# A gate joined behind its projection, memory tiles split in pairs, high and low parts by pairs of weight pieces

## The chip, the cores and the metric

The kernel runs on one core of a Trainium2 chip (trn2). The metric is the device time of one execution in microseconds; the median of several runs is given. TensorE (PE) does the matmuls and transposes, ScalarE (ACT) activations and copies, VectorE (DVE) elementwise work and reductions, SyncE (SP) issues the DMAs. Matmuls accumulate in PSUM, which is divided into banks.

## The reference

A decoder layer on 256 tokens of width 4096, in fp32. One input projection feeds three groups of heads, whose outputs are gated by SiLU, joined, projected, normalised and added to the residual.

```python
h = rms_norm(x, g_pre)
p = h @ w_in
p_shift = token_shift(p[..., :RWKV_SHIFT_WIDTH], mu_rwkv)
r, k, v, wl, al = jnp.split(p_shift, _offsets(RWKV_SHIFT_SPLITS), axis=-1)
g_rwkv, fq, fk, fv, f_logit, g_fox, mq, g_mq = jnp.split(p[..., RWKV_SHIFT_WIDTH:], _offsets(REST_SPLITS), axis=-1)
y_rwkv = rwkv7_branch(r, k, v, wl, al, w0, w_decay_up, a0, w_iclr_up, k_k, k_a, r_k, ln_x_w, ln_x_b)
log_f = jax.nn.log_sigmoid((f_logit + b_f).astype(jnp.float32)).transpose(0, 2, 1)
y_fox = fox_attention(to_heads(fq), to_heads(fk), to_heads(fv), log_f)
y_mem = memory_cross_attention(mq, mem, g_mem, w_mem_kv)
y = jnp.concatenate([y_rwkv * jax.nn.silu(g_rwkv), y_fox * jax.nn.silu(g_fox),
                     y_mem * jax.nn.silu(g_mq)], axis=-1)
y = y @ w_out
return x + rms_norm(y, g_post)
```

`rwkv7_branch` is a recurrence over the tokens for 24 heads of 64, with a norm for each head. `fox_attention` is causal softmax attention of 24 heads of 64 with a forget gate, and the memory attention has 4 heads of 256 over 256 memory tokens.

## The kernel before

**High and low parts.** Every operand of a big product is split into a high part (fp32r, a rounded copy) and a low part (what is left), so that a product is three matmul terms: high x high, high x low, low x high. `wsplit` (L211) loads a weight piece of 128 x 1024 by a DMA on SP's queue into one of four raw buffers, writes the high part `wh` on ACT (L217) and the low part `wl` on DVE (L218); each has three buffers.

**Projections.** `proj_t` makes 128 outputs of a projection for all 256 tokens, in 110 places of the program. Its 4096 inputs are 32 tiles of 128, its weights four pieces of eight tiles. The activations `xs` (`ms` for the memory) hold a tile's high and low part beside each other, so one matmul of 512 columns with `wh` (L248) gives two terms, and one of 256 columns with `wl` (L251) the third. For each piece come eight high matmuls and then eight low ones; in the last piece one high matmul stands at the very end, as it closes the sum. The sum stands in a PSUM tile of the pool `pj`, which has two banks. `join` adds its two halves: a copy on ACT (L262) and an addition on DVE (L264, or L266 where there is a scale); after that the bank is free.

**Names.** `pjq6400f` and `pjq7936f` are the banks of the query and key projections of a pair of fox heads, `pjgf` that of its gate, `pjgr` that of an RWKV gate; numbers behind the names are the pair (`f2`) or group and pair (`r02`). `pn` are the sums of `proj_n`, where the weights move and the activations stand (the memory values `pnmv`, the fox values, the output `pno`). `sf` are a pair's scores, `Lf` its logits and probabilities, `tf` and `of` the transposes and outputs; `mpr` and `vvr` are sums over a head for the RWKV norm; `yp` are the split tiles of the output projection's input, made from `y` (L896, L897).

**Order of the work.** After the memory phase (memory values, eight memory key projections `mk`, then queries and gates) come three groups of four pairs. A group runs four RWKV pairs, the recurrence, the fox values, and then fox pairs 0 to 3 with the norms between them: norms 0 and 1 are written behind fox pair 0, norm 2 behind fox pair 1, norm 3 behind fox pair 2. `rwkv_norm` (L732) sums the heads, projects the gate `gtr` and joins it into a tile with two buffers (tag `gt`); `put_y` (L339) reads the gate. The code is recorded in this order and a scheduler, which goes by its own estimate of each instruction's time, chooses the order on each engine when the program is built; weight loads and splits go ahead by a priority. On the chip each engine then works through its fixed order and waits by semaphores.

Of the kernel before, what the change touches and what calls it, by code (L numbers as in the profile page):

```python
# [8 lines left out]
F32 = mybir.dt.float32  # L9
F32R = mybir.dt.float32r  # L10
AF = mybir.ActivationFunctionType
ALU = mybir.AluOpType
# [3 lines left out]
P = 128  # L16
T = 256
D = 4096
KT = D // P
# [13 lines left out]
O_GR, O_FQ, O_FK, O_FV, O_FL, O_GF, O_MQ, O_GM = (  # L33
    4864, 6400, 7936, 9472, 11008, 11032, 12568, 13592)
# [110 lines left out]
def f32(ap):  # L145
    return ap.bitcast(F32)


class Layer:
# [86 lines left out]
    def proj_t(self, key, xs, name):  # L236

        nc = self.nc
        i = W_INDEX[key]
        ps = self.pj.tile([P, 512], F32, tag="pj", name=f"pj{name}")  # L240
        for j in range(4):
            with self.tc.high_priority(offset=self.ahead):
                wh, wl = self.wsplit(self.a["wT"][i, :, 8 * j:8 * j + 8, :], [P, 8, P], f"{name}_{j}")
            def mul(u, k):

                x = xs[(8 * j + k) // 2][:, (8 * j + k) % 2]
                if u == 0:
                    self.late = nc.tensor.matmul(ps, wh[:, k, :], x.rearrange("p u t -> p (u t)"),  # L248
                                                 start=(j == k == 0), stop=(j == 3 and k == 7))
                else:  # L250
                    nc.tensor.matmul(ps[:, 0:T], wl[:, k, :], x[:, 0, :], start=False, stop=False)  # L251


            last = j == 3
            for u, k in [(0, k) for k in range(8 - last)] + [(1, k) for k in range(8)] + [(0, 7)] * last:
                mul(u, k)
        return ps

    def join(self, ps, out, scale=1.0):
# [84 lines left out]
    def mem_phase(self):  # L344
        nc, tc, a = self.nc, self.tc, self.a
        with tc.tile_pool(name="pm", bufs=2) as pm:
            ms = [self.slot(f"m{i}") if i < 8 else
                  pm.tile([P, 2, 2, T], F32R, tag="ml", name=f"m{i}", bufs=8) for i in range(16)]

            def split(i, src, g, ds, rb):  # L350

                raw = pm.tile([P, 4, T], F32, tag="xraw", name=f"{g}raw{i}", bufs=3)
                nc.sync.dma_start(raw, src[:, 4 * i:4 * i + 4, :])
                if rb is not None:
                    for k in range(4):
                        m = nc.vector.scalar_tensor_tensor(raw[:, k, :], raw[:, k, :], self.prm(g, 4 * i + k), rb,
                                                           ALU.mult, ALU.mult)
                        self.behind(m, self.joined)
                for k in range(4):
                    sc = self.prm(g, 4 * i + k)  # L360
                    h, l = (ds[2 * i + k // 2][:, k % 2, u, :] for u in range(2))
                    if rb is None:
                        nc.scalar.activation(h, raw[:, k, :], AF.Copy, scale=sc)
                        nc.vector.scalar_tensor_tensor(l, raw[:, k, :], sc, f32(h), ALU.mult, ALU.subtract)
                    else:
                        nc.scalar.activation(h, raw[:, k, :], AF.Copy)
                        nc.vector.tensor_tensor(l, raw[:, k, :], f32(h), ALU.subtract)

            raw0 = [pm.tile([P, 4, T], F32, tag="xraw", name=f"firstraw{i}", bufs=3) for i in range(2)]

            def split_one(k, w):
# [7 lines left out]
                nc.vector.scalar_tensor_tensor(l, raw, sc, f32(h), ALU.mult, ALU.subtract)  # L379
                return h, l  # L380

            nc.scalar.dma_start(self.par, a["par"])
            mk = [pm.tile([P, 4, T], F32, name=f"mk{i}", bufs=1) for i in range(2)]
            mv = [pm.tile([P, 4, T], F32, name=f"mv{i}", bufs=1) for i in range(2)]
            ahead, self.ahead = self.ahead, 0
            for i in range(2):
                pre = (lambda kt: kt % 4 == 0 and split(kt // 4, a["memT"], "g_mem", ms, None)
                       ) if i == 0 else None
                ps = self.proj_n(a["wN"][i], ms, f"mv{i}", pre, i == 0, first=split_one if i == 0 else None)
                self.ahead = ahead  # L390
                for t in range(2):

                    o = mv[t].rearrange("p a b -> p (a b)")[:, 512 * i:512 * i + 512]
                    nc.scalar.activation(o, ps[t], AF.Copy)
# [11 lines left out]
            def x_piece(i):  # L406
                self.xs += [self.slot(f"x{2 * i}"), self.slot(f"x{2 * i + 1}")]
                split(i, a["xT"], "g_pre", self.xs, rxb)

            for i in range(8):  # L410
                ps = self.proj_t(("mem", 128 * i), ms, f"mk{i}")
# [8 lines left out]
            for h in range(4):  # L420
                q = pm.tile([P, 2, T], F32, tag="q", name=f"mq{h}", bufs=2)
                g = pm.tile([P, 2, T], F32, tag="g", name=f"mg{h}", bufs=2)
                for j in range(2):
                    ps = self.proj_t(("in", O_MQ + 256 * h + 128 * j), self.xs, f"mq{h}{j}")
                    self.join(ps, q[:, j, :], 1.0 / 16.0)
                for j in range(2):
                    ps = self.proj_t(("in", O_GM + 256 * h + 128 * j), self.xs, f"gm{h}{j}")
# [4 lines left out]
                for t in range(2):  # L432
                    for j in range(2):
                        c = 2 * h + j
                        nc.tensor.matmul(sv[:, t, :], q[:, j, P * t:P * t + P], mk[c // 4][:, c % 4, :],
                                         start=(j == 0), stop=(j == 1))
# [295 lines left out]
    def rwkv_norm(self, g, p, G, pr):  # L732

        nc = self.nc
        kp = GP * g + p
        n = f"r{g}{p}"
        Y, bv = G["Y"], G["bv"]

        def f(name, shape=(P, T)):
            return pr.tile(list(shape), F32, tag="f", name=f"{name}{n}", bufs=3)  # L740

        mp = self.head_sums(Y[:, p, :], f"mp{n}", "ch", pr, "f")
        yc = Y[:, p, :]
        nc.vector.scalar_tensor_tensor(yc, mp, -1.0 / HD, Y[:, p, :], ALU.mult, ALU.add)
        sq = f("ysq")
        nc.scalar.activation(sq, yc, AF.Square)

        gt = pr.tile([P, T], F32, name=f"gt{n}", tag="gt", bufs=2)
        gp = self.proj_t(("in", O_GR + 128 * kp), self.xs, f"g{n}")
        vp = self.head_sums(sq, f"vv{n}", "ch", pr, "f", self.late)  # L750
        self.join(gp, gt)
        nc.scalar.activation(gt, gt, AF.Silu)
        sd = f("sd")
        nc.scalar.activation(sd, vp, AF.Sqrt, bias=self.eps[:, 1:2], scale=1.0 / HD)
        nc.vector.reciprocal(sd, sd)
        nc.vector.tensor_tensor(yc, yc, sd, ALU.mult)
        nc.vector.tensor_scalar(yc, yc, self.prm("ln_x_w", kp), self.prm("ln_x_b", kp), ALU.mult, ALU.add)
        nc.vector.tensor_tensor(yc, yc, bv[p], ALU.add)
        self.put_y(kp, yc, gt, pr)
# [203 lines left out]
```

## Time and profile before

| what | value |
|---|---|
| time, median of 3 runs | 1980.67 us (1980.45 to 1981.16) |
| time of the profiled execution | 1980.58 us |
| its span in the trace | 1978.8 us |
| mean granted clock of TensorE | 0.996 of full |
| TensorE busy | 1955.3 us, 99% |
| DVE, ACT busy | 1324.5 us (67%), 1043.0 us (53%) |
| DMA moved | 382.75 MB, 193 GB/s on the mean |

The span is the stretch that the trace covers; 1.8 us of the execution lie around it. A busy engine is one that has an instruction running. The granted clock is TensorE's, as a share of its full 2.4 GHz.

### The profile page before, as it was taken

What the parts mean: (1) busy time and instruction counts of PE and PEld (TensorE: products, weight loads), DVE (VectorE), ACT (ScalarE), POOL (GpSimd) and SP (SyncE); (2) the same over time, 40 slices, a digit from 0 to 9 for tenths busy, and PEclk for the clock granted to TensorE, in tenths of its full rate; (3) what the DMA queues carried; (4) which work ended last, traced back from release to release, by engine and by line L of the source; (5) the groups of instructions that cost most, each with busy time, mean ns of one, the idle gap of its engine ahead of it and who ended that gap; (6) DMA issues with size and microseconds to landing.
All of it is one profiled execution on the core that took longest, in us unless ns stands there. A gap on an engine that the chain in (4) does not pass through costs nothing.

```text
span 1978.8 us, 30221 instructions
## 1 busy us (share of the span) xinstructions
PE 1955.3 (99%) x11772; PEld 1669.0 (84%) x11772; DVE 1324.5 (67%) x1904; ACT 1043.0 (53%) x1460; POOL 36.0 (2%) x138
## 2 busy tenths in 40 slices
PE   9999999999999999999999999999999999999997
PEld 7888888888888888888888888888888888888886
DVE  6467444458889656678897576778975675444445
ACT  7745544445554456565545565655445664444443
POOL 0000000000000000000000000000000001000000
PEclk9999999999999999999999999999999999999999
DMA  9966555665556555655565556556555578666665
GB/s 367 332 206 212 167 177 180 181 197 179 178 165 186 171 155 176 189 182 172 171 190 165 162 177 187 180 179 176 179 165 154 161 242 301 198 201 200 198 196 181
DMA packets 113283, 382.75 MB, mean 193 GB/s; under 512 B 12764, under 2 KB 19316, under 8 KB 113140
## 3 DMA queue, kind: packets, MB, share of 16 engines
q1 hardware_dynamic: 111204, 374.44, 61.1%
q0 software_dynamic: 1792, 6.29, 0.9%
q8 instruction: 92, 1.51, 0.3%
q14 instruction: 51, 0.42, 0.1%
q10 hardware_dynamic: 144, 0.10, 0.0%
HBM read 372.89 MB, written 7.89 MB: 192 GB/s over the span
## 4 chain that ended last, share of the span: by engine, by line
PE 97%; DMA 1%; DVE 1%; ACT 0%; issue 0%; SPq 0%; DVEq 0%; ACTq 0%
PE pno L284 6%; PE pno L285 6%; PE pno L283 6%; PE pjq7936f L248 5%; PE pjq6400f L248 5%; PE pjgf L248 5%; PE pjgr L248 5%; PE pjvr L248 4%; PE pjrr L248 4%; PE pjkr L248 4%; PE pjmq L248 3%; PE pjgm L248 3%; PE pjmk L248 3%; PE pjgr L251 2%; PE pjq7936f L251 2%; PE pjgf L251 2%
## 5 line engine op out<-in xcount | busy, mean ns | idle before, releaser
L218 DVE TENSOR_TENSOR wlno<-rawno,whno 128x1024 fp32r<-128x1024 f32 x128 | 156.6, 1225 | 161.6 <-ACT whno L217 161.6
L217 ACT ACTIVATE whno<-rawno 128x1024 fp32r<-128x1024 f32 x128 | 135.4, 1060 | 175.8 <-PE pno L285 167.3
L284 PE MATMUL pno<-wlno,yp 128*128 128x512 f32 x512 | 199.5, 390 | 0.5 <-DVE wlno L218 0.5
L285 PE MATMUL pno<-whno,yp 128*128 128x512 f32 x512 | 199.3, 389 | 0.0
L283 PE MATMUL pno<-whno,yp 128*128 128x512 f32 x512 | 180.2, 390 | 0.8 <-ACT whno L217 0.8
L284 PEld LDWEIGHTS pno<-wlno,yp 128*128 128x128 f32 x512 | 96.1, 188 | 21.3 <-DVE wlno L218 1.2
L283 PEld LDWEIGHTS pno<-whno,yp 128*128 128x128 f32 x512 | 96.0, 188 | 21.0 <-ACT whno L217 1.1
L285 PEld LDWEIGHTS pno<-whno,yp 128*128 128x128 f32 x512 | 96.1, 188 | 20.1
L248 PE MATMUL pjq7936f<-x,whq7936f 128*128 128x512 f32 x384 | 103.0, 401 | 7.5 <-DVE q6400f L266 7.5
L248 PE MATMUL pjgf<-x,whgf 128*128 128x512 f32 x384 | 101.6, 396 | 0.0
L248 PE MATMUL pjq6400f<-x,whq6400f 128*128 128x512 f32 x384 | 101.4, 396 | 0.0
L248 PE MATMUL pjvr<-x,whvr 128*128 128x512 f32 x384 | 100.9, 396 | 0.0
L248 PE MATMUL pjrr<-x,whrr 128*128 128x512 f32 x384 | 100.7, 392 | 0.0
L248 PE MATMUL pjgr<-x,whgr 128*128 128x512 f32 x384 | 100.6, 395 | 0.0
L248 PE MATMUL pjkr<-x,whkr 128*128 128x512 f32 x384 | 98.1, 392 | 0.0
L248 PEld LDWEIGHTS pjq7936f<-x,whq7936f 128*128 128x128 f32 x384 | 70.4, 192 | 20.8 <-DVE q6400f L266 8.1
L218 DVE TENSOR_TENSOR wlq7936f<-rawq7936f,whq7936f 128x1024 fp32r<-128x1024 f32 x48 | 58.7, 1222 | 42.3 <-ACT whq7936f L217 41.1
L218 DVE TENSOR_TENSOR wlkr<-rawkr,whkr 128x1024 fp32r<-128x1024 f32 x48 | 58.8, 1224 | 39.6 <-ACT whkr L217 36.1
L217 ACT ACTIVATE whrr<-rawrr 128x1024 fp32r<-128x1024 f32 x48 | 51.0, 1062 | 64.7 <-PE pjkr L248 57.8
L217 ACT ACTIVATE whq7936f<-rawq7936f 128x1024 fp32r<-128x1024 f32 x48 | 50.8, 1059 | 60.9 <-PE pjq6400f L248 33.8
L217 ACT ACTIVATE whkr<-rawkr 128x1024 fp32r<-128x1024 f32 x48 | 50.8, 1057 | 59.7 <-PE pjvr L248 54.4
L248 PEld LDWEIGHTS pjgf<-x,whgf 128*128 128x128 f32 x384 | 68.9, 189 | 15.4 <-issue 4.0
(371 smaller groups left out, 4561.6 us busy)
## 6 DMA issues: line engine op xcount, KB each, us to landing
rawno<-in_wO SPq DMA_DIRECT2D x128, 512.0 KB, 3.6
rawvr<-in_wT SPq DMA_DIRECT2D x48, 512.0 KB, 4.4
rawkr<-in_wT SPq DMA_DIRECT2D x48, 512.0 KB, 4.5
rawrr<-in_wT SPq DMA_DIRECT2D x48, 512.0 KB, 3.9
rawnfv<-in_wV SPq DMA_DIRECT2D x48, 512.0 KB, 3.6
rawq6400f<-in_wT SPq DMA_DIRECT2D x48, 512.0 KB, 4.2
rawq7936f<-in_wT SPq DMA_DIRECT2D x48, 512.0 KB, 4.1
rawgf<-in_wT SPq DMA_DIRECT2D x48, 512.0 KB, 4.2
```

Source lines behind the costliest of these rows:

```text
L217: nc.scalar.activation(wh, raw, AF.Copy)
L218: nc.vector.tensor_tensor(wl, raw, f32(wh), ALU.subtract)
L248: self.late = nc.tensor.matmul(ps, wh[:, k, :], x.rearrange("p u t -> p (u t)"), start=(j == k == 0), stop=(j == 3 and k == 7))
L251: nc.tensor.matmul(ps[:, 0:T], wl[:, k, :], x[:, 0, :], start=False, stop=False)
L283: nc.tensor.matmul(ps[t], xh, w[0][:, k, :], start=(kt == 0), stop=False)
L284: nc.tensor.matmul(ps[t], xh, w[1][:, k, :], start=False, stop=False)
L285: nc.tensor.matmul(ps[t], xl, w[0][:, k, :], start=False, stop=(kt == KT - 1))
```

## The change

There are three edits. In `proj_t` two weight pieces are loaded, and then come the sixteen high matmuls of both and the sixteen low ones (in the second pair the last high matmul stays at the end). In `rwkv_norm` the gate is joined, and put through SiLU, before the head sums of the squares, where it stood behind them. In the memory phase, the memory tiles behind the first eight are split two for each weight piece (`split_two`), where four were split for each second piece.

```diff
--- before.py
+++ after.py
@@ -238,22 +238,22 @@
         nc = self.nc
         i = W_INDEX[key]
         ps = self.pj.tile([P, 512], F32, tag="pj", name=f"pj{name}")
+        w = []
         for j in range(4):
             with self.tc.high_priority(offset=self.ahead):
-                wh, wl = self.wsplit(self.a["wT"][i, :, 8 * j:8 * j + 8, :], [P, 8, P], f"{name}_{j}")
-            def mul(u, k):
-
-                x = xs[(8 * j + k) // 2][:, (8 * j + k) % 2]
+                w.append(self.wsplit(self.a["wT"][i, :, 8 * j:8 * j + 8, :], [P, 8, P], f"{name}_{j}"))
+            if j % 2 == 0:
+                continue
+
+
+            hi = [(0, kt) for kt in range(8 * j - 8, 8 * j + 8)]
+            lo = [(1, kt) for _, kt in hi]
+            for u, kt in hi + lo if j == 1 else hi[:-1] + lo + hi[-1:]:
+                x, wk = xs[kt // 2][:, kt % 2], w[kt // 8][u][:, kt % 8, :]
                 if u == 0:
-                    self.late = nc.tensor.matmul(ps, wh[:, k, :], x.rearrange("p u t -> p (u t)"),
-                                                 start=(j == k == 0), stop=(j == 3 and k == 7))
+                    self.late = nc.tensor.matmul(ps, wk, x.rearrange("p u t -> p (u t)"), start=(kt == 0), stop=(kt == KT - 1))
                 else:
-                    nc.tensor.matmul(ps[:, 0:T], wl[:, k, :], x[:, 0, :], start=False, stop=False)
-
-
-            last = j == 3
-            for u, k in [(0, k) for k in range(8 - last)] + [(1, k) for k in range(8)] + [(0, 7)] * last:
-                mul(u, k)
+                    nc.tensor.matmul(ps[:, 0:T], wk, x[:, 0, :], start=False, stop=False)
         return ps
 
     def join(self, ps, out, scale=1.0):
@@ -351,20 +351,14 @@
 
                 raw = pm.tile([P, 4, T], F32, tag="xraw", name=f"{g}raw{i}", bufs=3)
                 nc.sync.dma_start(raw, src[:, 4 * i:4 * i + 4, :])
-                if rb is not None:
-                    for k in range(4):
-                        m = nc.vector.scalar_tensor_tensor(raw[:, k, :], raw[:, k, :], self.prm(g, 4 * i + k), rb,
-                                                           ALU.mult, ALU.mult)
-                        self.behind(m, self.joined)
                 for k in range(4):
-                    sc = self.prm(g, 4 * i + k)
+                    m = nc.vector.scalar_tensor_tensor(raw[:, k, :], raw[:, k, :], self.prm(g, 4 * i + k), rb,
+                                                       ALU.mult, ALU.mult)
+                    self.behind(m, self.joined)
+                for k in range(4):
                     h, l = (ds[2 * i + k // 2][:, k % 2, u, :] for u in range(2))
-                    if rb is None:
-                        nc.scalar.activation(h, raw[:, k, :], AF.Copy, scale=sc)
-                        nc.vector.scalar_tensor_tensor(l, raw[:, k, :], sc, f32(h), ALU.mult, ALU.subtract)
-                    else:
-                        nc.scalar.activation(h, raw[:, k, :], AF.Copy)
-                        nc.vector.tensor_tensor(l, raw[:, k, :], f32(h), ALU.subtract)
+                    nc.scalar.activation(h, raw[:, k, :], AF.Copy)
+                    nc.vector.tensor_tensor(l, raw[:, k, :], f32(h), ALU.subtract)
 
             raw0 = [pm.tile([P, 4, T], F32, tag="xraw", name=f"firstraw{i}", bufs=3) for i in range(2)]
 
@@ -379,13 +373,25 @@
                 nc.vector.scalar_tensor_tensor(l, raw, sc, f32(h), ALU.mult, ALU.subtract)
                 return h, l
 
+            held = {}
+
+            def split_two(kt):
+
+                if kt % 4 == 0:
+                    held[0] = pm.tile([P, 4, T], F32, tag="xraw", name=f"g_memraw{kt}", bufs=3)
+                    nc.sync.dma_start(held[0], a["memT"][:, kt:kt + 4, :])
+                for k in range(kt, kt + 2):
+                    raw, sc = held[0][:, k % 4, :], self.prm("g_mem", k)
+                    h, l = (ms[k // 2][:, k % 2, u, :] for u in range(2))
+                    nc.scalar.activation(h, raw, AF.Copy, scale=sc)
+                    nc.vector.scalar_tensor_tensor(l, raw, sc, f32(h), ALU.mult, ALU.subtract)
+
             nc.scalar.dma_start(self.par, a["par"])
             mk = [pm.tile([P, 4, T], F32, name=f"mk{i}", bufs=1) for i in range(2)]
             mv = [pm.tile([P, 4, T], F32, name=f"mv{i}", bufs=1) for i in range(2)]
             ahead, self.ahead = self.ahead, 0
             for i in range(2):
-                pre = (lambda kt: kt % 4 == 0 and split(kt // 4, a["memT"], "g_mem", ms, None)
-                       ) if i == 0 else None
+                pre = split_two if i == 0 else None
                 ps = self.proj_n(a["wN"][i], ms, f"mv{i}", pre, i == 0, first=split_one if i == 0 else None)
                 self.ahead = ahead
                 for t in range(2):
@@ -746,10 +752,9 @@
         nc.scalar.activation(sq, yc, AF.Square)
 
         gt = pr.tile([P, T], F32, name=f"gt{n}", tag="gt", bufs=2)
-        gp = self.proj_t(("in", O_GR + 128 * kp), self.xs, f"g{n}")
+        self.join(self.proj_t(("in", O_GR + 128 * kp), self.xs, f"g{n}"), gt)
+        nc.scalar.activation(gt, gt, AF.Silu)
         vp = self.head_sums(sq, f"vv{n}", "ch", pr, "f", self.late)
-        self.join(gp, gt)
-        nc.scalar.activation(gt, gt, AF.Silu)
         sd = f("sd")
         nc.scalar.activation(sd, vp, AF.Sqrt, bias=self.eps[:, 1:2], scale=1.0 / HD)
         nc.vector.reciprocal(sd, sd)
```

The order on the engines, first TensorE where the key projection `pjq7936f2` of fox pair 2 ends and the gate projection `pjgf2` begins, before the change:

```order
L251 MATMUL pjq7936f2_6969<-x15_1734,wlq7936f2_3_7039 128x256 x2
L248 MATMUL pjq7936f2_6969<-x15_1734,whq7936f2_3_7038 128x512
L248 MATMUL pjgf2_7068<-x0_1069,whgf2_0_7071 128x512 x2
L248 MATMUL pjgf2_7068<-x1_1070,whgf2_0_7071 128x512 x2
L248 MATMUL pjgf2_7068<-x2_1177,whgf2_0_7071 128x512 x2
L248 MATMUL pjgf2_7068<-x3_1178,whgf2_0_7071 128x512
L483 MATMUL vvr01_6417<-hvvr01_6413,blkr_81 128x256
L248 MATMUL pjgf2_7068<-x3_1178,whgf2_0_7071 128x512
```

and in the changed program (`mpr01` is a sum of the norm of pair 01, `sf20` and `sf21` are the scores of the two heads):

```order
L256 MATMUL pjq7936f2_6969<-x15_1734,wlq7936f2_3_7023 128x256 x2
L254 MATMUL pjq7936f2_6969<-x15_1734,whq7936f2_3_7022 128x512
L489 MATMUL mpr01_6317<-hmpr01_6313,blkr_81 128x256
L492 MATMUL mpr01_6317<-lmpr01_6314,blkr_81 128x256
L845 MATMUL sf20_7061<-q7936f2_7058,q6400f2_6966 128x128
L845 MATMUL sf21_7062<-q7936f2_7058,q6400f2_6966 128x128
L845 MATMUL sf20_7061<-q7936f2_7058,q6400f2_6966 128x256
L845 MATMUL sf21_7062<-q7936f2_7058,q6400f2_6966 128x256
L254 MATMUL pjgf2_7068<-x0_1069,whgf2_0_7071 128x512 x2
L254 MATMUL pjgf2_7068<-x1_1070,whgf2_0_7071 128x512 x2
L254 MATMUL pjgf2_7068<-x2_1177,whgf2_0_7071 128x512 x2
```

Before, the first matmul of the gate stood right behind the last of the key, and the scores some twenty rows later. Now the two sums and the four scores stand between them. The same holds at f6 and f10.

Second, ACT from the split of the key's last weight piece (`whq7936f2_3`) to a little behind its join, before:

```order
L217 ACTIVATE whq7936f2_3_7038<-rawq7936f2_3_7036 128x1024
L480 ACTIVATE hmpr01_6313<-Yr0_5367 128x256
L262 ACTIVATE gtr02_6766<-pjgr02_6767 128x256
L752 ACT_TABLE_LOAD
L752 ACTIVATE gtr02_6766<-gtr02_6766 128x256
L217 ACTIVATE whgf2_0_7071<-rawgf2_0_7069 128x1024
L746 ACTIVATE ysqr01_6321<-Yr0_5367 128x256
L217 ACTIVATE whgf2_1_7093<-rawgf2_1_7091 128x1024
L480 ACTIVATE hvvr01_6413<-ysqr01_6321 128x256
L217 ACTIVATE whgf2_2_7115<-rawgf2_2_7113 128x1024
L262 ACTIVATE q7936f2_7058<-pjq7936f2_6969 128x256
L217 ACTIVATE whgf2_3_7137<-rawgf2_3_7135 128x1024
```

and with the change, from the split of the gate's third piece (`whgf2_2`):

```order
L217 ACTIVATE whgf2_2_7115<-rawgf2_2_7113 128x1024
L262 ACTIVATE q7936f2_7058<-pjq7936f2_6969 128x256
L262 ACTIVATE gtr02_6766<-pjgr02_6767 128x256
L752 ACTIVATE ysqr01_6321<-Yr0_5367 128x256
L756 ACT_TABLE_LOAD
L756 ACTIVATE gtr02_6766<-gtr02_6766 128x256
L486 ACTIVATE hvvr01_6416<-ysqr01_6321 128x256
L866 ACT_TABLE_LOAD
L866 ACTIVATE Lf2_7160,smf2_7167<-Lf2_7160,mxf2_7166 128x128 x2
L866 ACTIVATE Lf2_7160,smf2_7167<-Lf2_7160,mxf2_7166 128x256 x2
L217 ACTIVATE whgf2_3_7121<-rawgf2_3_7119 128x1024
L217 ACTIVATE whgr03_0_7213<-rawgr03_0_7211 128x1024
```

The join of `gtr02` (`L262 ... gtr02<-pjgr02`) stood eight rows ahead of the key's join and now stands behind it; its SiLU, a second square and high half, and the four exponentials of `Lf2` come before the gate's last piece `whgf2_3`.

Third, ACT at the end of the mix, where the first pieces of the output weights (`whno0`) and the tiles `yp` are split, before:

```order
L896 ACTIVATE yp3_15685<-y1_15682 128x256 x2
L217 ACTIVATE whno0_2_15821<-rawno0_2_15819 128x1024
L262 ACTIVATE gf11_15539<-pjgf11_15540 128x256
L896 ACTIVATE yp4_15696<-y2_15694 128x256 x2
L896 ACTIVATE yp5_15697<-y2_15694 128x256 x2
L861 ACT_TABLE_LOAD
L861 ACTIVATE Lf11_15632,smf11_15639<-Lf11_15632,mxf11_15638 128x128 x2
L861 ACTIVATE Lf11_15632,smf11_15639<-Lf11_15632,mxf11_15638 128x256 x2
```

and with the change:

```order
L901 ACTIVATE yp3_15685<-y1_15682 128x256 x2
L866 ACT_TABLE_LOAD
L866 ACTIVATE Lf11_15632,smf11_15639<-Lf11_15632,mxf11_15638 128x128 x2
L866 ACTIVATE Lf11_15632,smf11_15639<-Lf11_15632,mxf11_15638 128x256 x2
L217 ACTIVATE whno0_2_15821<-rawno0_2_15819 128x1024
L262 ACTIVATE gf11_15539<-pjgf11_15540 128x256
L901 ACTIVATE yp4_15696<-y2_15694 128x256 x2
L901 ACTIVATE yp5_15697<-y2_15694 128x256 x2
L877 ACTIVATE ptf110_15653<-tf110_15649 128x384
```

The exponentials of the last pair (`Lf11`) stood behind the third piece `whno0_2` and two more tiles; now they stand ahead of them.

## Rows read from the trace of the kernel before

**Rows 1.** The page: chain of work that ended last, share of the span.

```profile
PE 97%; DMA 1%; DVE 1%; ACT 0%; issue 0%; SPq 0%; DVEq 0%; ACTq 0%
```

**Rows 2.** TensorE's waits: us in total, times, longest.

```profile
PE pjq7936f L248 <- DVE q6400f L266: 7.5, 3, 2.5
...
PE pno L283 <- ACT whno L217: 0.8, 1, 0.8
...
PE pno L284 <- DVE wlno L218: 0.5, 1, 0.5
```

**Rows 3.** Timeline at 735 to 738: start, duration, engine, line, [idle before, releaser].

```profile
735.23 1.06 ACT L217 ACTIVATE whq7936f<-rawq7936f 128x1024 fp32r<-128x1024 f32 x1 [2.05 <-PE pjq6400f L248]
736.19 0.37 ACT L262 ACTIVATE q6400f<-pjq6400f 128x256 f32<-128x256 f32 x1
736.32 1.23 DVE L218 TENSOR_TENSOR wlq7936f<-rawq7936f,whq7936f 128x1024 fp32r<-128x1024 f32 x1 [2.27 <-ACT whq7936f L217]
...
737.46 0.42 DVE L266 SCALAR_TENSOR_TENSOR q6400f<-pjq6400f,q6400f 128x256 f32<-128x256 f32 x1
...
737.93 2.77 PE L248 MATMUL pjq7936f<-x,whq7936f 128*128 128x512 f32 x8 [2.50 <-DVE q6400f L266]
```

**Rows 4.** Timeline at 742 to 754, the same group.

```profile
742.07 0.38 ACT L262 ACTIVATE gtr<-pjgr 128x256 f32<-128x256 f32 x1
...
744.08 0.42 ACT L752 ACTIVATE gtr<-gtr 128x256 f32<-128x256 f32 x1 [0.32 <-DVE gtr L264]
...
751.01 1.78 PE L248 MATMUL pjgf<-x,whgf 128*128 128x512 f32 x7
...
753.45 0.42 DVE L264 TENSOR_TENSOR q7936f<-pjq7936f,q7936f 128x256 f32<-128x256 f32 x1
```

**Rows 5.** Windows behind the three waits: stretch, busy by engine, clock, DMA.

```profile
737.93:740.50 2.57, 2.57 (x8) 2.04 (x9) 2.08 (x2) 0.42 (x1) 0.00 (x0) 0.74 0.66 186
740.50:742.20 1.70, 1.70 (x9) 1.69 (x8) 1.41 (x5) 1.46 (x3) 0.00 (x0) 0.50 0.07 27
...
1140.05:1142.20 2.15, 2.15 (x10) 1.78 (x11) 1.70 (x1) 0.42 (x1) 0.00 (x0) 1.00 0.66 179
...
1540.63:1543.70 3.07, 3.07 (x9) 2.40 (x10) 2.55 (x3) 0.42 (x1) 0.00 (x0) 0.61 0.57 171
1543.70:1545.10 1.40, 1.40 (x10) 1.40 (x9) 0.47 (x2) 1.18 (x2) 0.00 (x0) 0.65 0.00 0
```

**Rows 6.** Timeline of TensorE, start of the memory key projections.

```profile
96.27 1.98 PE L248 MATMUL pjmk<-m,whmk 128*128 128x512 f32 x8
98.08 1.12 PE L251 MATMUL pjmk<-m,wlmk 128*128 128x256 f32 x8
99.03 2.00 PE L248 MATMUL pjmk<-m,whmk 128*128 128x512 f32 x8
100.88 1.11 PE L251 MATMUL pjmk<-m,wlmk 128*128 128x256 f32 x8
101.83 2.00 PE L248 MATMUL pjmk<-m,whmk 128*128 128x512 f32 x8
103.67 1.12 PE L251 MATMUL pjmk<-m,wlmk 128*128 128x256 f32 x8
```

**Rows 7.** Timeline at the end of the mix, 1613 to 1621.

```profile
1613.57 1.34 ACT L896 ACTIVATE yp<-y 128x256 fp32r<-128x256 f32 x4 [1.44 <-DMA y<-yd]
...
1614.62 0.40 PE L283 MATMUL pno<-whno,yp 128*128 128x512 f32 x1
...
1617.42 1.28 ACT L861 ACT_TABLE_LOAD   x1
...
1620.62 0.18 DVE L863 RECIPROCAL smf<-smf 128x4 f32<-128x4 f32 x1 [1.44 <-ACT Lf L861]
```

**Rows 8.** Line L251 by form: min/median/max ns, first and last start.

```profile
L251 PE MATMUL pjmk<-m,wlmk x256: 277/283/283, 98.1 to 185.3; 128*128 128x256 f32 x128
```

## The prediction

> **What bounds the kernel now.** I read the page first: in the chain that ended last TensorE holds 97% [rows 1], so a change is worth what it gives TensorE to wait for, or takes away, and what it changes in TensorE's own pace. Next the list of TensorE's waits [rows 2]. After the start only two kinds are left: 7.5 us in three pieces, before the first matmul of the key projections `pjq7936f`, for the DVE half of the query's join (L266); and 0.8 + 0.5 us at the seam to the output projection. Third, the timeline around one of the three [rows 3] and the windows behind all three [rows 5]: there the granted clock falls. Fourth, the timeline of an undisturbed run of projections, for the pace of high and low matmuls [rows 6]. The profiled execution took 1980.58 us, span 1978.8, and the median shown is 1980.67, so the two agree and I add to 1980.6.
>
> **The three waits.** In group 0 the bank `pjq7936f2` needs is the one that `pjq6400f2` has just filled, because the other holds `pjgr02` until its late join at 742.07 [rows 4]. So TensorE waits for a chain: weight split 1.06 on ACT, the ACT half of the join, a low part of 1.23 on DVE, and the DVE half at 737.46; TensorE starts at 737.93 after 2.50 idle [rows 3]. The next projection, `pjgf2`, waits for nothing: it starts at 751.01 in the other bank, which `gr02` has left, while the join of the key goes on until 753.45 + 0.42 = 753.87 [rows 4].
>
> **Gate joined right behind its projection.** The order shows that this does not happen for `gr02`. `gt` has two buffers, so the join must wait until the norm of pair 00 has read its gate. ACT's queue in the changed program has `gtr02` behind the join of `q7936f2`, where before it stood ahead of it by eight rows. The bank that `gr02` holds is therefore not free when `pjgf2` wants one, and TensorE's queue shows the answer: the four score matmuls `sf2`, which need the joined key, now stand ahead of `pjgf2`, and that takes the key's bank. The wait of `q7936f2` stays as it is, and a second one like it comes behind it. The same order is there for f6 and f10, and nowhere else; three new waits. The price has a row: in the kernel before the key's join ended 753.87 - 751.01 = 2.86 us after TensorE was free to go on [rows 4], plus 0.05 to start, as 737.88 to 737.93 [rows 3]. Two small matmuls of the next norm (`mpr01`, 0.23 us together) are done meanwhile. So 2.6 to 2.7; the existing wait shows 2.50. I take 2.6, three times: **+7.8** (bounds 2.3 and 2.9: 6.9 to 8.7). Queued behind the waiting matmul is the whole of TensorE; ACT and DVE get ahead in that time, so nothing is owed to them later.
>
> **What follows such a wait.** Behind the first and third wait the granted clock is 0.74, 0.50 and 0.61, 0.65 of full, so part of it at the 1.2 GHz level; behind the second it is 1.00 [rows 5]. Eight high and eight low matmuls take 1.84 + 0.95 = 2.79 undisturbed [rows 6]; behind the waits they took 2.57 + 1.70 = 4.27, 2.15 + 0.95 = 3.10 (the low run there undisturbed), and 3.07 + 1.40 = 4.47: 1.5, 0.3 and 1.7 too much, mean 1.15. The new waits are as long, so 3 x 1.15: **+3.5** (0 to 5). Another follower: the split of the last piece of `gf2` now stands on ACT behind the gate's join and silu, a square, a high half, two table loads and four exponentials. The join is 0.38, the silu 0.42 [rows 4], the square and the high half have the silu's size, the table loads 2 x 1.28, the exponentials 1.9 (from a table load's end at 1618.70 to the reciprocal at 1620.62) [rows 7], with the split of 1.06 in all 7.2; TensorE wants the piece some 8.2 after the scores start (0.8 + 3.7 + 1.9 + 1.8). What DVE's share of the softmax adds may make it up to 1.5 late each time, less where the clock is low anyway. Value 0, bound +4.5.
>
> **High then low by pairs.** A projection went high 8, low 8, four times; now high 16, low 16, twice. Nothing is removed; fewer changes from low to high are left. Eight high matmuls behind `pn` matmuls, which are as wide, take 98.08 - 96.27 = 1.81; behind a low run 100.88 - 99.03 = 1.85 and 103.67 - 101.83 = 1.84 [rows 6]: 0.03 too much. A low run's first start to its last end is 1.12, one alone is 0.283 [rows 6, 8], so the seven steps inside are 0.120, and the step to the high one is 0.95 - 0.84 = 0.11: where two low runs are joined 0.01 is lost. Net 0.02 a change. Counted over the order, changes from low to high go from 430 to 209, 221 fewer: **-4.4** (bounds 0 and -6.6, if nothing is lost). Each part has three buffers. Counted from a pair's start, the buffer of its first high part comes free at 1.8 us, and the piece that follows in it is wanted at 7.4; that of its first low part comes free at 4.6, its follower is wanted at 10. With 1.06 and 1.23 for a split [rows 3] these are covered; cost 0. If that cover were gone, 110 projections would each pay some tenths.
>
> The Trainium skill speaks against this gain ("TensorE: Matmul & The Clock Gate", "Back-to-back issue gap"): the isolated gap depends on the columns of one matmul alone, N / 2.4 + 2.5 ns. By it high is 216 and low 109 ns in any order, and this term is 0; the rows are 227 (1.81 / 8) and 120, and differ by what ran before, so the measurement decides. By the rule the sum is that of the second rival below.
>
> **Memory tiles two per piece.** Engine by engine, ACT, DVE and SP stand in the old order until well into the first `mk` projection: the splits still go four together. Cost and gain 0.
>
> **The seam at the end of the mix.** In the last pair the scores come earlier, but exponentials move ahead of the third output piece's split on ACT, and the transposes `tf110` up from behind 36 output matmuls to behind 13. Estimate, from rows 7 and 3: the second tile's split on ACT ends 1613.57 + 1.34 = 1614.9, table load 1.28, exponentials 1.9, reciprocal and scaling 0.7: 1618.8. TensorE is there at 1614.62 + 13 x 0.227 = 1617.6: waits 1.2. The third piece's high part then ends at 1619.2, its low part 1.22 later, TensorE wanted it at 1619.2: 1.2. Eighteen output matmuls, `tf111` and `of11` on, at 1626.4, the fourth piece, behind the third to fifth tiles' splits (1.34 each), the table load and two copies, ends at about 1627.3: 0.9, and its low part 0.75 more. Together 4.0, less the 0.82 and 0.52 of today [rows 2]: **+2.7** (0 to 4).
>
> **Sum.** 7.8 + 3.5 - 4.4 + 2.7 = +9.6: 1990.2 us.
>
> **The rivals.** *Slower as above*: chance 0.60, own range 1986 to 1994. *The order of high and low is free*: the 0.03 belongs to something that stays, say to a weight piece's first matmuls, of which there are as many as before; no -4.4, so 1994.6. For it speaks that a new weight piece begins with each high run as rows 6 have them, against it that the low runs, which change pieces too, are not slowed; 0.15. The Trainium skill's rule above gives the same. *The new wait at full clock and a harmless seam*: 7.8 - 4.4 = +3.4, 1984.0; for it the 1.00 behind one wait in three [rows 5]; 0.13. *Late pieces*: a pair wants two pieces at its start, and if ACT is late by 0.1 us in each of 110 projections, +11 more, 2001; against it the slack above; 0.05. *Faster*: the gate's early join frees the second bank. Were `gtr02` joined before 734.80, both the old waits and their slow stretches would go: -7.5 - 3.5 - 4.4, 1965.2. It decides where the norm's gate buffer comes free before the query's projection ends; in the order its ACT half stands behind the key's join, some 17 us too late. With the smaller form, no new wait paid and only -4.4, 1976.2, 0.07.
>
> **How the numbers follow.** Within 0.2% (4 us, about what a measurement here can tell from no change) is 1976.7 to 1984.6: half of the third rival and a little of the last, 0.11; faster 0.06; slower 0.83. The range of 8 in 10 runs from 1983 (the third rival) to 1997 (the second with late pieces at `gf`).
>
> **What would show it.** Right: six waits of TensorE for joins instead of three, the new ones on `sf`, 2.4 to 2.7 each; a granted clock under 0.8 behind some; sixteen high matmuls in 3.66, not 2 x 1.84; waits for `Lf`, `whno`, `wlno` near 1618 to 1628. Wrong: no wait ahead of `sf`; high runs of sixteen at 3.68, or waits of projections for `wh` or `wl`.

## The result, and the profile after

The changed kernel takes 1995.49 us (median of 6, 1994.38 to 2000.67) against 1981.2 for the kernel before (6 runs): a ratio of 1.0078, with a 95% interval of 1.0068 to 1.0088. It is slower by 14 us where +9.6 was forecast, inside the range. Of the runs reported below one execution, of the kernel with the memory tiles alone, took 2761.4 us at a granted clock of 0.65; the time given for that kernel is the median of its nine others. The profiled execution took 1995.26 us; its page begins so:

```profile
span 1993.5 us, 30252 instructions
...
PE 1960.2 (98%) x11772; PEld 1674.2 (84%) x11772; DVE 1322.9 (66%) x1904; ACT 1039.5 (52%) x1460; POOL 36.6 (2%) x138
```

The span has grown by 14.7 us and TensorE's busy time by 4.9, so some 10 are waits. The list of TensorE's waits of the changed kernel (us in total, times, longest) answers to [rows 2]:

```profile
PE vvr L489 <- ACT hvvr L486: 6.5, 3, 2.2
PE mpr L492 <- DVE lmpr L487: 3.4, 3, 1.1
PE sf L845 <- DVE q7936f L264: 3.3, 3, 1.1
PE zpr L673 <- DVE Enr L661: 1.8, 3, 0.7
PE pno L283 <- ACT whno L217: 1.7, 1, 1.7
PE pno L284 <- DVE wlno L218: 1.2, 1, 1.2
...
PE pjq7936f L254 <- DVE q6400f L266: 0.4, 2, 0.2
```

The three waits of before are still there; they are only put down to the small matmul `vvr` that now stands in front of the key projection (6.5, and 0.4 at the key itself, for the 7.5 of before). New are three waits in two pieces each, on `mpr` and on `sf`, 2.2 us together, and one on `zpr` in each recurrence. The timeline of the changed kernel from the end of the query to the gate at f2 answers to [rows 3, 4]:

```profile
736.90 0.39 PE L489 MATMUL vvr<-hvvr,blkr 128*128 128x256 f32 x1 [2.17 <-ACT hvvr L486]
...
737.33 0.42 DVE L487 TENSOR_TENSOR lvvr<-ysqr,hvvr 128x256 fp32r<-128x256 f32 x1
...
737.47 5.53 PE L254 MATMUL pjq7936f<-x,whq7936f 128*128 128x512 f32 x16 [0.18 <-DVE q6400f L266]
...
743.31 0.28 PE L492 MATMUL vvr<-lvvr,blkr 128*128 128x256 f32 x1
...
750.19 0.39 PE L254 MATMUL pjq7936f<-x,whq7936f 128*128 128x512 f32 x1
...
751.04 0.42 DVE L339 TENSOR_TENSOR yt<-Yr,gtr 128x256 f32<-128x256 f32 x1
...
751.59 0.37 ACT L262 ACTIVATE q7936f<-pjq7936f 128x256 f32<-128x256 f32 x1
...
751.85 0.38 ACT L262 ACTIVATE gtr<-pjgr 128x256 f32<-128x256 f32 x1
752.86 0.42 DVE L264 TENSOR_TENSOR q7936f<-pjq7936f,q7936f 128x256 f32<-128x256 f32 x1
...
753.33 0.93 PE L845 MATMUL sf<-q7936f,q6400f 64*128 64x128 f32 x8 [1.10 <-DVE q7936f L264]
```

The reader is to see one chain in it. The low half of `vvr`'s input is ready at 737.75, but the matmul that sums it stands behind sixteen high and four low ones of the key and runs at 743.31. So the norm reads its gate (`yt`, L339) only at 751.04, 9.4 us later than before:

```profile
741.61 0.42 DVE L339 TENSOR_TENSOR yt<-Yr,gtr 128x256 f32<-128x256 f32 x1
```

Of the 9.4, 3.7 are there already when DVE has the sum's low half ready (737.75 for 734.05), the stand behind the run adds 4.5 (5.6 for 1.1), and 1.3 come up on ACT and DVE behind the sum. The join of the other gate (`gtr`, 751.85) follows, and it is behind the key's (751.59). TensorE ended the key at 750.42, and goes on with the scores at 753.33: 2.9 later, of which 0.24 are the `mpr` matmuls.

Sixteen high matmuls at 737.47 took 5.4 us, to 742.83, where 3.63 are due, and the granted clock fell here too. The windows of the changed kernel behind a wait (columns as in [rows 5]):

```profile
740.00:742.80 2.80, 2.80 (x11) 2.26 (x10) 0.00 (x0) 1.06 (x1) 0.00 (x0) 0.76 0.03 12
753.30:758.00 4.70, 4.67 (x25) 3.72 (x26) 2.48 (x8) 3.71 (x5) 0.00 (x0) 1.00 0.59 205
1142.00:1147.40 5.40, 5.37 (x30) 4.72 (x31) 0.59 (x2) 2.46 (x3) 0.00 (x0) 1.00 0.33 105
...
1158.00:1161.00 3.00, 3.00 (x8) 2.30 (x7) 1.86 (x5) 2.31 (x4) 0.00 (x0) 0.50 0.43 152
1547.40:1550.00 2.60, 2.60 (x6) 2.08 (x7) 0.21 (x1) 0.00 (x0) 0.00 (x0) 0.50 0.65 202
...
1564.00:1567.00 3.00, 3.00 (x8) 2.32 (x8) 1.87 (x6) 2.97 (x4) 0.00 (x0) 0.50 0.68 203
```

At f2 it is low behind the first wait and full behind the second, at f6 the other way round, and at f10 it is 0.50, the 1.2 GHz level, behind both. The starts of the same projection in both timelines show where the 14.7 us came up:

| start of | before | after | later by | came up since |
|---|---|---|---|---|
| `mk0` | 96.27 | 96.64 | 0.4 | 0.4 |
| `vr`, group 0 | 411.45 | 411.08 | -0.4 | -0.7 |
| key at f2 | 737.93 | 737.47 | -0.5 | -0.1 |
| `vr`, group 1 | 811.91 | 814.03 | 2.1 | 2.6 |
| `vr`, group 2 | 1212.49 | 1219.50 | 7.0 | 4.9, of it 5.0 from the key at f6 on |
| key at f10 | 1540.63 | 1547.33 | 6.7 | -0.3 |
| `pno` | 1614.62 | 1626.18 | 11.6 | 4.9 |
| end of the span | 1978.8 | 1993.5 | 14.7 | 3.1 |

From the keys of pairs 2, 6 and 10 to the next group come 2.6, 5.0 and 4.9 us, from the seam 3.1; everything else together gains 0.9. The pace of high and low, to be set beside [rows 6]:

```profile
96.64 3.79 PE L254 MATMUL pjmk<-m,whmk 128*128 128x512 f32 x16
100.27 2.08 PE L256 MATMUL pjmk<-m,wlmk 128*128 128x256 f32 x16
102.18 3.59 PE L254 MATMUL pjmk<-m,whmk 128*128 128x512 f32 x15
105.61 2.08 PE L256 MATMUL pjmk<-m,wlmk 128*128 128x256 f32 x16
```

Sixteen high matmuls behind `pn` take 3.63, 0.227 each, and fifteen behind a low run 3.43, 0.025 over 15 x 0.227. The excess is about one for each change, as before, and there are half as many changes. The seam's timeline answers to [rows 7]:

```profile
1628.09 1.28 ACT L866 ACT_TABLE_LOAD   x1
...
1629.13 0.50 PE L284 MATMUL pno<-wlno,yp 128*128 128x512 f32 x1 [1.19 <-DVE wlno L218]
...
1631.15 1.04 ACT L217 ACTIVATE whno<-rawno 128x1024 fp32r<-128x1024 f32 x1
1631.28 0.18 DVE L868 RECIPROCAL smf<-smf 128x4 f32<-128x4 f32 x1 [1.53 <-ACT Lf L866]
...
1632.25 0.80 PE L283 MATMUL pno<-whno,yp 128*128 128x512 f32 x1 [1.68 <-ACT whno L217]
```

and a window behind the second of these waits:

```profile
1633.00:1635.00 2.00, 2.00 (x8) 1.50 (x7) 2.00 (x7) 1.97 (x7) 0.00 (x0) 0.50 0.62 137
```

The exponentials (table load at 1628.09 to the reciprocal at 1631.28) hold the third piece `whno` back to 1631.15; TensorE waits 1.68 for it, and then runs at a granted clock of 0.50 until 1635. The wait of 1.19 ahead of it is for the second piece's low part, which could be made from 1625.66 on, when its high part was there, but stands on DVE behind the maxima of the softmax (`mxf`) and two `yp` tiles until 1627.86.

### The profile page after: what moved, and what is told of

It is laid out like the page before. It is cut to its first block, busy times and chain, and to the rows that moved or that the text cites. A ratio compares the mean times of both kernels' runs of the same rounds, so it can differ in the third digit from the quotient of the medians.

```text
span 1993.5 us, 30252 instructions
## 1 busy us (share of the span) xinstructions
PE 1960.2 (98%) x11772; PEld 1674.2 (84%) x11772; DVE 1322.9 (66%) x1904; ACT 1039.5 (52%) x1460; POOL 36.6 (2%) x138
## 5 line engine op out<-in xcount | busy, mean ns | idle before, releaser
L254 PE MATMUL pjq7936f<-x,whq7936f 128*128 128x512 f32 x384 | 97.8, 402 | 0.5 <-DVE q6400f L266 0.4
L254 PE MATMUL pjrr<-x,whrr 128*128 128x512 f32 x384 | 95.1, 391 | 0.0
L254 PE MATMUL pjq6400f<-x,whq6400f 128*128 128x512 f32 x384 | 94.4, 391 | 0.0
L254 PE MATMUL pjvr<-x,whvr 128*128 128x512 f32 x384 | 94.3, 391 | 0.0
L254 PE MATMUL pjkr<-x,whkr 128*128 128x512 f32 x384 | 93.5, 391 | 0.0
L254 PEld LDWEIGHTS pjgf<-x,whgf 128*128 128x128 f32 x384 | 73.0, 194 | 17.8 <-issue 2.0
L254 PEld LDWEIGHTS pjkr<-x,whkr 128*128 128x128 f32 x384 | 71.4, 188 | 13.7
L254 PEld LDWEIGHTS pjrr<-x,whrr 128*128 128x128 f32 x384 | 71.4, 188 | 13.4
```

What stands on the lines that cost most here:

```text
L254: self.late = nc.tensor.matmul(ps, wk, x.rearrange("p u t -> p (u t)"), start=(kt == 0), stop=(kt == KT - 1))
```

## The experiments

**Which edit makes the second wait.** The prediction put it down to the gate's join (theory A). The rival, theory B, is that the pair order does it. Three kernels have one edit each; the diffs are the three parts of the change. The pair order alone:

> Only the pair order of high and low parts; gate join and memory tiles as before. Theory A (the gate's join right behind its projection moves gtr02 behind the key's join, as the prediction said): no second bank wait, so about 1981 - 4 + 3 = 1980 us. Theory B (the pair order alone moves it; the order of this kernel shows the gate projection of pairs 2, 6 and 10 in the key's bank, as in the changed kernel): three waits on sf of 2.2 us and some half clock, about 1995 us, the same as the changed kernel.

Measured: 1998.84 us, ratio 1.0082 (1.0067 to 1.0097). Its waits of TensorE are those of the changed kernel:

```profile
PE vvr L483 <- ACT hvvr L480: 6.5, 3, 2.2
PE mpr L486 <- DVE lmpr L481: 3.4, 3, 1.1
PE sf L840 <- DVE q7936f L264: 3.3, 3, 1.1
```

Behind the second wait at f2, where the changed kernel kept the full clock, a window of this run has 0.52:

```profile
754.00:757.00 3.00, 3.00 (x8) 2.35 (x8) 1.73 (x5) 2.48 (x4) 0.00 (x0) 0.52 0.45 142
```

The gate's join alone:

> Only the gate's join and SiLU moved ahead of the head sums. Theory A: the second wait of 2.7 us at f2, f6 and f10 and its half clock, about 1981 + 12 = 1993 us. Theory B: the bank use stays that of the kernel before, three waits of 2.5 us and no more, 1981 us within 2.

Measured: 1982.07 us, ratio 1.0002 (0.9993 to 1.0012). Its waits are those of [rows 2], with none on `sf`:

```profile
PE pjq7936f L248 <- DVE q6400f L266: 7.5, 3, 2.5
```

The memory tiles alone:

> Only the memory tiles split two per weight piece. Both theories: the order on ACT and DVE stays, 1981 us within 1. If the start is worth something by itself (the changed trace is 0.5 us ahead at its first memory matmul and 0.4 us behind by the key projections), it shows here as 0.3 us, below what the runs can tell.

Measured: 1981.39 us, ratio 1.0002 (0.9992 to 1.0012). Theory A falls: the pair order by itself costs what the whole change costs, and the other two edits cost and give nothing that can be measured.

**Is it the held bank.** The gate's tile gets a place in a ring of eight tiles that the RWKV pairs use and the norms leave idle, so that its join need not wait for the norm of pair 00:

```diff
-        gt = pr.tile([P, T], F32, name=f"gt{n}", tag="gt", bufs=2)
+        gt = pr.tile([P, T], F32, name=f"gt{n}", tag="e", bufs=8)
```

In the changed kernel:

> The changed kernel with the norm's gate tile in the ring of eight e tiles in place of two of its own, so that the join need not wait for the norm of pair 00. If the held bank is the cause of both waits (theories A and B): no wait for q6400f or q7936f, no half clock behind them, about 1995.5 - 12.7 for the second waits and their clock - 8 for the first ones, less 2 of half clock there: 1971 to 1975 us. If the waits come from something else (late pieces of a pair, SP's queue): no change, 1995 us.

Measured: 1970.79 us, ratio 0.9944 (0.9929 to 0.9959), 25 us under the changed kernel. No wait for a query's or a key's join is left:

```profile
PE pno L283 <- ACT whno L217: 2.7, 1, 2.7
PE zpr L673 <- DVE Enr L661: 2.0, 3, 0.7
```

The same line in the kernel before:

> The kernel before with the norm's gate tile in the ring of eight e tiles, nothing else. If the held bank is what its three waits cost: 7.5 us of idle, half a microsecond for the matmuls that drain ahead of them and about 3 of half clock go, 1981 - 11 = 1970 us, with no wait for q6400f. If only the idle time itself counted: 1973.5.

Measured: 1969.41 us, ratio 0.9941 (0.9929 to 0.9954). The three waits of [rows 2] are gone, and in windows of 4 us over the same places the granted clock stays full:

```profile
737.00:741.00 4.00, 4.00 (x28) 3.64 (x27) 3.04 (x4) 3.55 (x4) 0.00 (x0) 1.00 0.46 143
1136.00:1140.00 4.00, 4.00 (x24) 3.46 (x23) 3.19 (x3) 3.03 (x4) 0.00 (x0) 1.00 0.74 230
1535.00:1539.00 4.00, 4.00 (x25) 3.55 (x24) 3.44 (x4) 2.22 (x4) 0.00 (x0) 1.00 0.65 215
```

So a wait of 2.5 us cost about 4 here, counting what follows it: 12 us for three.

**What the pair order is worth without the bank.** With that ring, the pair order alone:

> The pair order alone, with the gate tile in the ring of eight, to be set against the run with the old order and the same ring. If a change from low to high costs 0.018 to 0.02 us, the order gains 4 and the seam takes 2.6 back and the recurrence's new wait up to 2: 1 us either way of the old order with that ring, 1969 to 1971. If the order of high and low were free: 3 to 5 us slower than it, 1973 to 1975.

Measured: 1968.63 us, ratio 0.9940 (0.9928 to 0.9952), which can't be told from the order by eights (eight high, then eight low, as before) with the same ring. In the traces the pair order is 0.04 us a projection ahead. Between the fox values and the key of pair f2, where the recurrence runs, it loses 0.5 of its lead, though ten projections there should add 0.4, and its list of waits shows where most of that goes:

```profile
PE pno L283 <- ACT whno L217: 2.7, 1, 2.7
PE zpr L667 <- DVE Enr L655: 2.0, 3, 0.7
```

The wait for the DVE's transposes (`zpr`) and the longer one at the seam are not in the list of the kernel by eights with the ring, where the waits at the seam are 0.9 and 1.3. Why DVE is later there no run shows.

**Does a change from low to high cost.** Each piece in quarters, four high, four low, four high, four low, with the ring. The trace then has 871 places where a low matmul of a projection is followed at once by a high one, in place of 427:

```diff
-            for u, k in [(0, k) for k in range(8 - last)] + [(1, k) for k in range(8)] + [(0, 7)] * last:
+            for u, k in ([(0, k) for k in range(4)] + [(1, k) for k in range(4)] + [(0, k) for k in range(4, 8 - last)]
+                         + [(1, k) for k in range(4, 8)] + [(0, 7)] * last):
```

> As the kernel before with the gate tile in the ring of eight, but each weight piece as four high, four low, four high, four low: some 440 more changes from low to high and nothing else. If a change costs 0.018 to 0.02 us: 8 to 9 us slower than with eights, about 1978. If it is free: the same, 1970. If it is the start of a new weight piece that costs: the same, 1970.

Measured: 1978.24 us, ratio 0.9986 (0.9977 to 0.9995), 8.8 over the eights with the ring. Only part of it is the pace:

```profile
96.70 1.07 PE L248 MATMUL pjmk<-m,whmk 128*128 128x512 f32 x4
97.60 0.64 PE L251 MATMUL pjmk<-m,wlmk 128*128 128x256 f32 x4
98.08 1.09 PE L248 MATMUL pjmk<-m,whmk 128*128 128x512 f32 x4
99.00 0.63 PE L251 MATMUL pjmk<-m,wlmk 128*128 128x256 f32 x4
```

Four high matmuls take 0.90 behind `pn` and 0.92 behind a low run. From one `mk` projection to the next the quarters lose 0.04 to 0.05 us against the eights, for four changes more: 0.011 a change, about 5 us in 110 projections. From the first `pno` matmul to the end of the span it loses 3.6 more, where TensorE waits 2.3 and 1.9 us for the output pieces. The changes do cost, within one weight piece, so it is not the piece's start; the Trainium skill's rule for the isolated gap, which goes by the columns alone ("TensorE: Matmul & The Clock Gate", "Back-to-back issue gap"), doesn't hold for this mix.

**The seam.** The changed kernel with the ring, and the last pair's gate projection by single pieces, so that its exponentials stand behind the third output piece again:

```diff
+            step = 1 if name == f"gf{NPAIR - 1}" else 2
-            if j % 2 == 0:
+            if (j + 1) % step:
                 continue
-            hi = [(0, kt) for kt in range(8 * j - 8, 8 * j + 8)]
+            hi = [(0, kt) for kt in range(8 * (j + 1 - step), 8 * j + 8)]
...
-            for u, kt in hi + lo if j == 1 else hi[:-1] + lo + hi[-1:]:
+            for u, kt in hi + lo if j < 3 else hi[:-1] + lo + hi[-1:]:
```

> The changed kernel with the gate tile in the ring of eight, and the gate projection of the last fox pair by single pieces again, which puts the exponentials of that pair behind the third output piece on ACT as before. If the order at the seam is what costs there: the 2.6 us of the seam come back, 1968 us. If the seam's cost comes from the pairs being faster ahead of it: unchanged, 1970.8.

Measured: 1967.79 us, ratio 0.9935 (0.9923 to 0.9948): 3.0 under the changed kernel with the ring, but only 0.8 under the pair order with the ring, which was timed beside it. The waits at the seam fall from 2.7 to

```profile
PE pno L284 <- ACT whno L217: 0.6, 1, 0.6
PE pno L285 <- DVE wlno L218: 0.5, 1, 0.5
```

So some of the seam's cost does come from the order there, 1.6 us by these waits. From the first `pno` matmul to the end of the span the changed kernel with the ring took 366.7 us, this one 364.1 and the kernel before 364.2, so in the traces the 2.6 are back. The times alone can't show it, since the start of the first memory key projection, ahead of all this, differs by 2.4 us between the two traces (95.89 and 98.29). It is the fastest kernel here, but those with the ring at 1968.63 and 1969.41 us lie inside its interval.

**How the pair order makes the norm late.** The timeline above names the low half of `vvr`. In the changed kernel, with two buffers for the gate as it was, one order is added:

```diff
+                    if kt == 0 and name in (f"q{O_FK}f2", f"q{O_FK}f6", f"q{O_FK}f10"):
+                        self.behind(self.late, self.vlo)
...
```

`vlo` is that low half's matmul in the first norm of each group.

> The changed kernel, with one order added: the first high matmul of the key projections of pairs 2, 6 and 10 stands behind the low half of the head sum vvr of the first norm. In the changed kernel that half stands behind sixteen high matmuls and four low ones of the key, 5.5 us after it could run, and the norm, the gate's buffer and the join of gtr02 are late by it; in this kernel's order gtr02's join is ahead of the key's again and pjgf2 has a bank of its own. If this is what makes the second wait: no wait on sf, three waits of 2.2 to 2.7 ahead of the key as in the kernel before, 1981 - 4 + 3 + 1 = 1980 to 1983 us. If the second wait has another cause in the pair order: 1995 us.

Measured: 1986.49 us, ratio 1.0031 (1.0019 to 1.0044), 9 us under the changed kernel. The timeline shows the chain put right:

```profile
736.87 0.39 PE L494 MATMUL vvr<-lvvr,blkr 128*128 128x256 f32 x1 [0.51 <-DVE lvvr L489]
...
741.02 0.42 DVE L341 TENSOR_TENSOR yt<-Yr,gtr 128x256 f32<-128x256 f32 x1
...
741.60 0.36 ACT L264 ACTIVATE gtr<-pjgr 128x256 f32<-128x256 f32 x1
...
750.05 1.09 PE L254 MATMUL pjgf<-x,whgf 128*128 128x512 f32 x4
```

The sum runs at 736.87, the norm reads its gate at 741.02, the join of `gtr` comes at 741.60, and the gate projection starts in its own bank at 750.05. No wait on `sf` or `mpr` is left. It stays 3.5 us above the upper end of what was expected: the sum itself now waits for DVE (0.5 us, three times), and behind each of the three waits the granted clock fell, 0.57, 0.55 and 0.52 in windows of 3 to 4 us, where in the kernel before it fell behind two.

## Why the prediction was right, and where it was not

**The second bank wait** was the main term and is what happened: three waits, 2.9 us from the key's end to the scores, 2.67 of them lost, for the 2.6 forecast. But the step that named its cause failed. "Gate joined right behind its projection" was charged with it, since the order of the whole change has `gtr02` behind the key; the gate edit alone leaves the order and the time as they were, and the pair order alone makes the wait. The order of a whole change doesn't say which edit moved a row. The runs show the way: a run of sixteen high matmuls that the scheduler did not break stands ahead of a small sum, the sum's norm is late by 9 us, and the gate buffer with it.

**The clock behind a wait** had +3.5 for three waits. From the key on, the three groups lost 2.6, 5.0 and 4.9, the wait of 2.67 and the clock behind the first and the second wait together: 12.5 for the 11.3 of both terms. It fell behind four of the six waits, where before it fell behind two of three. Behind which wait it falls differed between runs of like kernels, so that the size of this term came out near is luck. The late pieces, put at 0 with a bound of 4.5, were 0: no wait of `proj_t` for `wh` or `wl` is in the list.

**High then low by pairs** had -4.4. The pace is as forecast, 0.04 us a projection, and sixteen high matmuls take the 3.66 that were named as a sign (3.43 + 0.23). What failed is the step that set the cost of the rest to nothing: the buffers did cover the splits, but DVE's chain in the recurrence came later to `zpr` (0.67 us of waiting in each group), and outside the keys' stretches and the seam only 0.9 us was left as a gain, the start's 0.4 counted against it: 1.3 of pace and waits where 4.4 were forecast. Of the 3.1 that are missing some 0.7 lie in the keys' stretches, which hold six projections each, 1.8 are the waits for `zpr`, and 0.6 stay open.

**The seam** had +2.7 and cost 3.1. The mechanism was right in part: the exponentials ahead of the third piece cost a wait of 1.7. The other wait, 1.2, was not for the softmax, as the sum had it, but for the second piece's low part on DVE; two more waits didn't come, and a slow stretch that the sum did not have did. That the size agrees is partly luck. **The memory tiles** had 0, and 0 was found.

**The signs.** Six waits for joins came instead of three, but each new one in two pieces, on `mpr` and on `sf`, 2.2 us of idle together and not 2.4 to 2.7 on `sf`.

**The rivals.** That order is free is refuted by the quarters. The faster rival had the right mechanism in the wrong place: the early join does free both waits, as the ring of eight shows, but for that it is the gate's buffer that must be free, not the place of the join in the code. By the profile 14.7 us came instead of 9.6: 3.1 of the difference is the gain that was missing, 1.2 the keys' stretches, 0.4 the seam and 0.4 the start, which differs by as much from run to run.

## What to carry to other kernels

A kernel that is bound by one engine, with two accumulators in turn, stops where one of them waits for a buffer that another chain frees; the cure is the buffer, and here a place in an idle ring was worth 12 us, more than any order. Longer uninterrupted runs on the bound engine save at each change but delay the small instructions that other chains wait for; look at what stands behind a run. Build each edit by itself before its cost is charged to it.

## What the runs showed of the hardware

A run of high matmuls of 512 columns behind a run of 256-column ones with other weights takes 0.025 us more than the same run undisturbed, whether it is of eight or of sixteen, and 0.02 more when it is of four. In the memory key projections of the kernel before, the starts of single matmuls put this on the first five of a run, 0.233, 0.235, 0.228, 0.233 and 0.231 us for 0.227, while the first step of the low run behind it is 0.113 for 0.120; so the change there and back costs 0.02, as two fewer of them gained 0.04 a projection.

After idle stretches of 2.2 to 2.5 us on TensorE, and after two of 1.1 us parted by one small matmul, the granted clock fell to 0.50 for 2 to 3 us in some cases and stayed at 1.00 in others. At f2's second wait it was 1.00 in the changed kernel and 0.52 in the pair order alone. With the three waits of the kernel before gone it stayed at 1.00 in the windows over the same places.
